# Sample states of a retention layer: keys and values of all batches in each 32-row quarter, updates by four 32-row matmuls

## The chip, the cores and the metric

The kernel runs on one core of one Trainium2 chip. The metric is the device time of one execution in microseconds (us), the median of several. TensorE is called PE in the profile, VectorE DVE, ScalarE ACT, GpSimd POOL; SP issues the DMAs.

## The reference

One layer of a decoder runs on 256 prompt tokens and on 8 sample batches of 4 new tokens each, so that 288 columns of tokens go through every product. The part that the change touches is the retention branch, for 8 heads with keys of 256 and values of 512 features. Each sample batch has a state of 256 x 512 per head, which is read, used and written back:

```python
inner = jnp.einsum('bhij,bhje->bhie', scores, v)
cross = jnp.einsum('bhid,bhde->bhie', q, S) * jnp.exp(log_g[:, None] * (i + 1.0))[None, :, :, None]
k_dec = k * jnp.exp(log_g[:, None] * (C - 1.0 - i))[None, :, :, None]
S_new = jnp.exp(log_g * C)[None, :, None, None] * S + jnp.einsum('bhjd,bhje->bhde', k_dec, v)
return S_new, inner + cross
```

For a sample batch C is 4. All else of the layer (projections, short convolution, output product, convolutional feed-forward) is dense products of 2048 or 5632 features with the 288 columns.

## The kernel before

Tokens lie on the free dimension and features on partitions. Every weight is loaded as float32, a unit of 1 MB at a time (`wunit`, L71), and split into two float32r parts, `wh` by ACT (L83) and `wl` by DVE (L84); a product then takes three matmuls of 128 rows, 128 columns and 288 streamed columns (`mm3`, L91 to L94). One unit is 48 such products. Three units of raw weights are held at a time.

The retention branch goes head by head (L516 to L541). Beside the projections of head h run the steps of `tail` of head h - 1 (L501): eight steps for the sample states, then their outputs, the gate and the product with `p_ret`. The program is given to a scheduler that fixes the order on each engine ahead of time; on the chip each engine takes its instructions strictly in that order.

For the samples of one head there are these parts:

- `krep` and the last 128 columns of `vT` hold the keys and values of the 32 sample tokens four times over. Transposed they give `ks` (L381) and `vs` (L362), 128 rows each: four quarters of 32 rows, each with all 8 batches. The quarters differ in being the high or the low part of the number, so that one matmul over 128 rows adds all four products of the parts.
- `state_cross` (L434) works on four batches at once: for each of the four and for each half `dt` of the key features, one float32 matmul of 128 rows and 32 columns, streaming 512 columns of the state, into its own 32 partitions of `pso`. The four have their own 32 columns of the array each.
- `spad` (L443) adds the scores' part to `pso` with one 128-row matmul.
- `state_update` (L445), for one batch: ACT copies `ks` to `kb` with a mask that keeps the rows of that batch (L448), PE makes two matmuls `pu` of 128 rows and 512 streamed columns (L451), DVE adds each to the decayed state (L452), and SP stores the state.
- `state_batch` (L456) loads four states ahead, runs `state_cross` at batches 0 and 4, and loads batch b + 4 when batch b is done. The state tiles `st` have five buffers (`NST`, L34), so a load for batch 5, 6 or 7 waits for an earlier store.

PSUM has three buffers with the tag `acc`, for the dense products, and five with the tag `r`, for all else: `pso` holds one of those five from the first cross product to the end of the head's samples, and the `pu` tiles use the others.

Of the kernel before, what the change touches and what calls it, by code (L numbers as in the profile page):

```python
# [34 lines left out]
J = 4  # L35
# [16 lines left out]
def tile_hybrid_step(ctx: ExitStack, tc: tile.TileContext, a, o):  # L52
# [83 lines left out]
    def rstd_tokens(sq, name):  # L136
        """1/sqrt(mean over features + eps) of each token, tokens on partitions"""
        st = psum("r", f"st_{name}")
        for c, at, _, _ in CHUNKS:
            T.matmul(st[:, c : c + 1], sq[:, at : at + P], mean, start=True, stop=True)  # L140
        tt = cp.tile([P, 3], F32, tag="stt", name=f"stt_{name}", bufs=2)
        V.tensor_scalar(out=tt, in0=st[:, 0:3], scalar1=EPS, scalar2=None, op0=ALU.add)
        r = cp.tile([P, 3], F32, tag="str", name=f"str_{name}", bufs=2)
        G.tensor_tensor(out=r, in0=tt, in1=mhalf[:, 0:3], op=ALU.pow)
        return r

    def rstd_bcast(r, name):
        """that, of all tokens on every partition (in PSUM)"""
        dg = cp.tile([P, N], F32, tag="stdg", name=f"stdg_{name}")
        rb = psum("r", f"strb_{name}")  # L150
        for c, _, n, skip in CHUNKS:
            to = slice(P * c, P * c + n)
            V.tensor_scalar(out=dg[:, to], in0=ident[:, skip:], scalar1=r[:, c : c + 1],
                            scalar2=None, op0=ALU.mult)
            T.matmul(rb[:, to], ones, dg[:, to], start=True, stop=True)  # L155
        return rb[:, :N]

# [67 lines left out]
    # ======================= retention =======================  # L225
    # The sample states of a head stream beside the projections of the next one.
# [4 lines left out]
    bmask = sp.tile([P, DEC_B], F32, name="bmask")  # L231
    nc.sync.dma_start(out=bmask, in_=a["bmask"])
    # batch g * J + j: its queries at columns 4g of block (g, j), its outputs in rows 32j + 4g
# [8 lines left out]
    def toks(t):  # L242
        return t.rearrange("p (g j t) -> p g j t", g=G2, j=J)

# [35 lines left out]
    def qk_split(hd):  # L280
        h, rot = hd.h, hd.rot
        hd.qkh = ap_.tile([P, 4, SEQ], F32R, tag="ph", name=f"qkh{h}")
        hd.qkl = ap_.tile([P, 4, SEQ], F32R, tag="pl", name=f"qkl{h}")
        S.copy(hd.qkh, rot[:, :, :SEQ])
        V.tensor_tensor(out=hd.qkl, in0=rot[:, :, :SEQ], in1=hd.qkh.bitcast(F32), op=ALU.subtract)
        hd.krep = ap_.tile([P, 2, 4, NS], F32, tag="krep", name=f"krep{h}")
        S.copy(hd.krep, rot[:, 2:4, SEQ:].unsqueeze(2).to_broadcast([P, 2, 4, NS]))

    def v_unit(hd, e):
        """v, scaled; the samples' part four times, for its exact parts."""  # L290
        if e == 0:
            hd.vT = ap_.tile([P, 4, SEQ + 4 * NS], F32, tag="vT", name=f"vT{hd.h}")
        acc = project(32 + 4 * hd.h + e, f"a_v{hd.h}_{e}")
        V.tensor_tensor(out=hd.vT[:, e, :SEQ], in0=acc[:, :SEQ], in1=rstd1[:, :SEQ], op=ALU.mult)
        V.tensor_tensor(
            out=hd.vT[:, e, SEQ:].rearrange("p (r n) -> p r n", r=4),
            in0=acc[:, SEQ:N].unsqueeze(1).to_broadcast([P, 4, NS]),
            in1=rstd1[:, SEQ:N].unsqueeze(1).to_broadcast([P, 4, NS]), op=ALU.mult,
        )

    def g_unit(hd, e):
        """silu(g) doubled, as (tanh(g/2) + 1) * g"""
        h = hd.h
        acc = project(64 + 4 * h + e, f"a_g{h}_{e}")
        gr = ap_.tile([P, N], F32, tag="gr", name=f"gr{h}_{e}")
        V.tensor_tensor(out=gr, in0=acc[:, :N], in1=rstd1, op=ALU.mult)
        th = ap_.tile([P, N], F32, tag="th", name=f"th{h}_{e}")
        S.activation(th, gr, AF.Tanh, scale=0.5)
        sge = sp.tile([P, N], F32, tag="sg", name=f"sg{h}_{e}", bufs=4)
        V.scalar_tensor_tensor(out=sge, in0=th, scalar=1.0, in1=gr, op0=ALU.add, op1=ALU.mult)  # L310
        hd.sg.append(sge)

    def scores(hd):
        """transposed, [j, i], with the decay"""
# [12 lines left out]
        for dt in range(2):  # L327
            T.matmul(scs[:, :NS], hd.krep[:, dt].rearrange("p r n -> p (r n)"), rot[:, dt, SEQ:],
                     start=dt == 0, stop=dt == 1)
# [10 lines left out]
        for q in (1, 3):  # L340
            r = slice(32 * q, 32 * q + 32)
            V.tensor_tensor(out=rows(spad)[r], in0=toks(sms)[r], in1=rows(spad)[r].bitcast(F32),
                            op=ALU.subtract)

    def q_pad(hd):
        """the samples' queries with their decay, one batch per block, zeros elsewhere"""
        h, rot = hd.h, hd.rot
        for g in range(G2):
            at = J * DEC_T * g
            V.tensor_tensor(  # L350
                out=qpad[:, :, g, :, DEC_T * g : DEC_T * g + DEC_T],
                in0=rot[:, 0:2, SEQ + at : SEQ + at + J * DEC_T].rearrange("p d (j t) -> p d j t", j=J),
                in1=qdec[:, h, at : at + J * DEC_T].rearrange("p (j t) -> p j t", j=J)
                .unsqueeze(1).to_broadcast([P, 2, J, DEC_T]), op=ALU.mult,
            )

    def v_trans(hd):
        """v with tokens on partitions"""
# [4 lines left out]
        for c in range(3):  # L363
# [7 lines left out]
            else:  # L371
                S.copy(hd.vs, tp)
                V.tensor_tensor(out=hd.vs[64:, :], in0=tp[64:, :], in1=hd.vs[64:, :].bitcast(F32),
                                op=ALU.subtract)

    def k_trans(hd):
        """k with tokens on partitions, and its decay to the end of the step"""
# [3 lines left out]
        hd.ks = sp.tile([P, DK], F32R, tag="ks", name=f"ks{h}")  # L381
        for c in range(3):
            tp = psum("r", f"tk{h}_{c}")
            for dt in range(2):
                src = hd.rot[:, 2 + dt, P * c : P * c + P] if c < 2 else hd.krep[:, dt].rearrange("p r n -> p (r n)")
# [6 lines left out]
            else:  # L392
                S.activation(hd.ks, tp[:, :DK], AF.Copy, scale=dec)
                for q in (1, 3):
                    r = slice(32 * q, 32 * q + 32)
                    V.scalar_tensor_tensor(out=hd.ks[r, :], in0=tp[r, :DK], scalar=dec[r],
                                           in1=hd.ks[r, :].bitcast(F32), op0=ALU.mult, op1=ALU.subtract)

    def prompt_out(hd):
        """outputs of the prompt, normalised per head"""  # L400
# [33 lines left out]
    def state_cross(hd, g):  # L434
        """what the states of J batches add to their outputs, side by side in the array"""
# [9 lines left out]
    def state_update(hd, b):  # L445
        h, st = hd.h, hd.st[b]
        kb = sp.tile([P, DK], F32R, tag="kb", name=f"kb{h}_{b}", bufs=2)
        S.activation(kb, hd.ks.bitcast(F32), AF.Copy, scale=bmask[:, b : b + 1])  # L448
        for dt in range(2):
            pu = psum("r", f"pu{h}_{b}{dt}")  # L450
            T.matmul(pu, kb[:, P * dt : P * dt + P], hd.vs, start=True, stop=True)  # L451
            V.scalar_tensor_tensor(out=st[:, dt, :], in0=st[:, dt, :], scalar=float(G_STEP[h]),  # L452
                                   in1=pu, op0=ALU.mult, op1=ALU.add)
        nc.sync.dma_start(out=o["ret_s"][h, b], in_=st)

    def state_batch(hd, b):  # L456
        if b == 0:
            for j in range(J):
                state_load(hd, j)
        if b % J == 0:  # L460
            state_cross(hd, b // J)
        state_update(hd, b)
        if b + J < DEC_B:
            state_load(hd, b + J)
# [9 lines left out]
    def gated(hd):  # L474
        """back to features on partitions, gated"""
# [12 lines left out]
    def p_ret_unit(hd, g):  # L488
        """this head's part of four columns of p_ret"""
# [11 lines left out]
    def tail(hd):  # L501
        """the rest of a head, in steps to go beside other products"""
        for b in range(DEC_B):
            yield lambda b=b: state_batch(hd, b)
# [39 lines left out]
    # ======================= phase B: gated short conv, merge =======================  # L544
# [92 lines left out]
    # ======================= phase C: w_o, residual =======================  # L637
# [33 lines left out]
    # the first products of the channel mixer go along with its inputs  # L671
# [61 lines left out]
    # ======================= phase D: conv FFN =======================  # L733
# [74 lines left out]
def _constants():  # L808
# [11 lines left out]
    row = np.arange(P) % NS  # L820
    for h in range(H):
# [10 lines left out]
    bmask = (b[row][:, None] == np.arange(DEC_B)[None, :]).astype(np.float32)  # L832
    return {
        "cos": np.cos(ang).astype(np.float32), "sin": np.sin(ang).astype(np.float32),
        "mask": mask, "kdec": kdec, "qdec": qdec, "bmask": bmask,
# [82 lines left out]
```

## Time and profile before

| | |
|---|---|
| three runs | 2568.78, 2570.11, 2570.53 us; median 2570.11 us |
| profiled execution, its span from first to last instruction | 2568.1 us |
| PE busy | 2536.6 us of the span |
| DVE busy | 1542.1 us |
| ACT busy | 1069.1 us |
| DMA | 474.18 MB, 185 GB/s mean |

The profile gives no time of the profiled execution but its span; the three runs stand 0.7 to 2.4 us above it. A PE record in the trace has a start and a modelled end: since matmuls follow each other in a pipeline, the time that one costs is read from the distance between its start and the start of the next, not from its duration. A float32 matmul (as in `state_cross`) has two records, a float32r matmul one.

### The profile page before, as it was taken

The numbers are of one execution on the slowest core, as the hardware profiler recorded it, in microseconds if no ns is written. First come the engines' busy times: TensorE is split into PE (matmuls) and PEld (weight loads), VectorE is DVE, ScalarE is ACT, GpSimd is POOL, SyncE is SP. The second block draws the span as 40 slices with busy tenths as digits, with TensorE's granted clock in tenths as the row PEclk, the third lists the DMA queues.
The fourth block names the chain that finished last, engine by engine and source line by source line (L and its number), as shares of the span: only waits on it lengthen the run. The fifth ranks groups of instructions, "written<-read, shape, count | busy, mean of one in ns | idle before, by whom it ended". The sixth has DMA issues, their size and how long they took to land. (4 is left out here: it accounts for less than half of the span.)

```text
span 2568.1 us, 44840 instructions
## 1 busy us (share of the span) xinstructions
PE 2536.6 (99%) x18864; PEld 2485.6 (97%) x18864; DVE 1542.1 (60%) x2349; ACT 1069.1 (42%) x1475; POOL 86.9 (3%) x244
## 2 busy tenths in 40 slices
PE   8999999999999999999999999999999999999997
PEld 8999999999999999999999999989999999999997
DVE  7565656666665656555555555477666446666644
ACT  5444444443444433333333333454444334444443
POOL 2000000000000000000000000021000000000001
PEclk9999999999999999999999999999999999999998
DMA  7565565656575746444444445434444455444453
GB/s 268 176 233 210 211 225 203 219 203 229 191 249 180 266 164 221 165 165 166 168 171 170 165 164 200 166 132 172 165 166 160 160 167 185 168 165 164 150 169 117
DMA packets 85163, 474.18 MB, mean 185 GB/s; under 512 B 10464, under 2 KB 13280, under 8 KB 43360
## 3 DMA queue, kind: packets, MB, share of 16 engines
q1 hardware_dynamic: 84960, 471.30, 52.3%
q8 instruction: 148, 2.42, 0.4%
q14 instruction: 55, 0.45, 0.1%
HBM read 430.60 MB, written 40.66 MB: 184 GB/s over the span
## 5 line engine op out<-in xcount | busy, mean ns | idle before, releaser
L83 ACT CAST wh<-raw 128x1024 fp32r<-128x1024 f32 (+2 forms) x776 | 778.7, 1004 | 1275.3 <-PE a_d L93 160.4
L84 DVE TENSOR_TENSOR wl<-raw,wh 128x1024 fp32r<-128x1024 f32 (+2 forms) x776 | 907.0, 1169 | 665.8 <-ACT wh L83 662.5
L93 PE MATMUL a_d<-fop,wh 128*128 128x288 f32 x704 | 209.1, 297 | 0.0
L92 PE MATMUL a_d<-fop,wh 128*128 128x288 f32 x704 | 208.4, 296 | 0.0
L94 PE MATMUL a_d<-fop,wl 128*128 128x288 f32 x704 | 206.3, 293 | 0.0
L92 PE MATMUL a_gate<-h2op,wh 128*128 128x288 f32 x688 | 203.2, 295 | 0.0
L94 PE MATMUL a_gate<-h2op,wl 128*128 128x288 f32 x688 | 202.1, 294 | 1.0 <-DVE wl L84 1.0
L93 PE MATMUL a_gate<-h2op,wh 128*128 128x288 f32 x688 | 202.3, 294 | 0.0
L92 PE MATMUL a_up<-h2op,wh 128*128 128x288 f32 x672 | 198.5, 295 | 0.0
L93 PE MATMUL a_up<-h2op,wh 128*128 128x288 f32 x672 | 197.6, 294 | 0.0
L94 PE MATMUL a_up<-h2op,wl 128*128 128x288 f32 x672 | 197.3, 294 | 0.0
L92 PE MATMUL a_g<-hop,wh 128*128 128x288 f32 x512 | 152.6, 298 | 0.0
L92 PE MATMUL a_p<-yop,wh 128*128 128x288 f32 x512 | 152.5, 298 | 0.0
L93 PE MATMUL a_g<-hop,wh 128*128 128x288 f32 x512 | 152.2, 297 | 0.0
L92 PE MATMUL a_v<-hop,wh 128*128 128x288 f32 x512 | 151.3, 295 | 0.0
L92 PE MATMUL a_gt<-hop,wh 128*128 128x288 f32 x512 | 151.2, 295 | 0.0
L93 PE MATMUL a_p<-yop,wh 128*128 128x288 f32 x512 | 151.0, 295 | 0.0
L94 PE MATMUL a_p<-yop,wl 128*128 128x288 f32 x512 | 150.8, 295 | 0.0
L94 PE MATMUL a_g<-hop,wl 128*128 128x288 f32 x512 | 150.7, 294 | 0.0
L93 PE MATMUL a_gt<-hop,wh 128*128 128x288 f32 x512 | 150.5, 294 | 0.0
L93 PE MATMUL a_v<-hop,wh 128*128 128x288 f32 x512 | 150.5, 294 | 0.0
L94 PE MATMUL a_v<-hop,wl 128*128 128x288 f32 x512 | 150.4, 294 | 0.0
(270 smaller groups left out, 6636.0 us busy)
## 6 DMA issues: line engine op xcount, KB each, us to landing
raw<-in_w_in SPq DMA_DIRECT2D x173, 1024.0 KB, 4.9
raw<-in_w_down SPq DMA_DIRECT2D x64, 704.0 KB, 4.1
raw<-in_w_up SPq DMA_DIRECT2D x43, 1024.0 KB, 4.8
raw<-in_w_gate SPq DMA_DIRECT2D x43, 1024.0 KB, 4.8
st<-in_state SPq DMA_DIRECT2D x64, 512.0 KB, 3.7
out_ret_s<-st SPq DMA_DIRECT2D x64, 512.0 KB, 6.3
raw<-in_p_ret SPq DMA_DIRECT2D x32, 1024.0 KB, 4.8
raw<-in_p_conv SPq DMA_DIRECT2D x16, 1024.0 KB, 4.8
```

What stands on the lines that cost most here:

```text
L83: S.copy(wh[:, to], raw[:, of])
L84: V.tensor_tensor(out=wl[:, to], in0=raw[:, of], in1=wh[:, to].bitcast(F32), op=ALU.subtract)
L92: T.matmul(out, lh, rh, start=first, stop=False)
L93: T.matmul(out, lh, rl, start=False, stop=False)
L94: T.matmul(out, ll, rh, start=False, stop=last)
```

## The change

The samples' tokens are laid out anew on the 128 rows. Before, quarter r of the array (rows 32r to 32r + 31) held copy r of all 32 tokens. Now quarter j holds, in four blocks of 8 rows, the four copies of the tokens of batches j and 4 + j, 4 rows each. So the four copies of one batch, with the high and low parts, lie in one quarter. The constants on the host follow (`kdec`, the samples' part of `mask`), and `rmask` takes the place of `bmask`: two columns that choose high or low part, two that choose the batches 0 to 3 or 4 to 7.

- `krep` is filled by four ACT copies in place of one, and the samples' part of `vT` by two DVE products per tile in place of one.
- the low parts of `spad`, `vs` and the keys are made with `rmask` on all rows.
- `kb` is made once for each group of four batches in `k_trans` (two tiles per head, beside the tile `kd`), not once per batch. `ks` is gone.
- an update is a matmul of 32 rows, 128 columns and 512 streamed columns. The number of update matmuls stays 16 per head, 128 in all.
- `state_step` replaces `state_batch`: step 0 loads the states of batches 0 to 3 and makes the first cross products, step 2 updates all four batches, stores them and loads batches 4 to 7, step 4 makes the second cross products, step 6 the second updates and stores.

```diff
-        hd.krep = ap_.tile([P, 2, 4, NS], F32, tag="krep", name=f"krep{h}")
-        S.copy(hd.krep, rot[:, 2:4, SEQ:].unsqueeze(2).to_broadcast([P, 2, 4, NS]))
+        hd.krep = ap_.tile([P, 2, J, 4, G2, DEC_T], F32, tag="krep", name=f"krep{h}")
+        for dt in range(2):
+            for g in range(G2):
+                S.copy(hd.krep[:, dt, :, :, g, :], batches(rot[:, 2 + dt, SEQ:], g))
...
-                S.activation(hd.ks, tp[:, :DK], AF.Copy, scale=dec)
-                for q in (1, 3):
-                    r = slice(32 * q, 32 * q + 32)
-                    V.scalar_tensor_tensor(out=hd.ks[r, :], in0=tp[r, :DK], scalar=dec[r],
-                                           in1=hd.ks[r, :].bitcast(F32), op0=ALU.mult, op1=ALU.subtract)
+                kd = ap_.tile([P, DK], F32, tag="kd", name=f"kd{h}")
+                S.activation(kd, tp[:, :DK], AF.Copy, scale=dec)
+                S.copy(hd.kb[0], kd)
+                V.scalar_tensor_tensor(out=kd, in0=hd.kb[0].bitcast(F32), scalar=rmask[:, 0:1], in1=kd,
+                                       op0=ALU.mult, op1=ALU.add)
+                for g in range(G2):
+                    S.activation(hd.kb[g], kd, AF.Copy, scale=rmask[:, 2 + g : 3 + g])
...
-    def state_update(hd, b):
-        h, st = hd.h, hd.st[b]
-        kb = sp.tile([P, DK], F32R, tag="kb", name=f"kb{h}_{b}", bufs=2)
-        S.activation(kb, hd.ks.bitcast(F32), AF.Copy, scale=bmask[:, b : b + 1])
+    def state_update(hd, g):
+
+        h = hd.h
         for dt in range(2):
-            pu = psum("r", f"pu{h}_{b}{dt}")
-            T.matmul(pu, kb[:, P * dt : P * dt + P], hd.vs, start=True, stop=True)
-            V.scalar_tensor_tensor(out=st[:, dt, :], in0=st[:, dt, :], scalar=float(G_STEP[h]),
-                                   in1=pu, op0=ALU.mult, op1=ALU.add)
-        nc.sync.dma_start(out=o["ret_s"][h, b], in_=st)
...
+            pus = []
+            for j in range(J):
+                pu = psum("r", f"pu{h}_{g}{dt}{j}")
+                r = slice(32 * j, 32 * j + 32)
+                T.matmul(pu, hd.kb[g][r, P * dt : P * dt + P], hd.vs[r, :], start=True, stop=True)
+                pus.append(pu)
+            for j, pu in enumerate(pus):
+                st = hd.st[J * g + j]
+                V.scalar_tensor_tensor(out=st[:, dt, :], in0=st[:, dt, :], scalar=float(G_STEP[h]),
+                                       in1=pu, op0=ALU.mult, op1=ALU.add)
+
+    def state_step(hd, i):
+
+        if i == 0:
             for j in range(J):
                 state_load(hd, j)
-        if b % J == 0:
-            state_cross(hd, b // J)
-        state_update(hd, b)
-        if b + J < DEC_B:
-            state_load(hd, b + J)
+        if i in (0, 4):
+            state_cross(hd, i // 4)
+        if i in (2, 6):
+            state_update(hd, i // 4)
+            for j in range(J):
+                nc.sync.dma_start(out=o["ret_s"][hd.h, J * (i // 4) + j], in_=hd.st[J * (i // 4) + j])
+        if i == 2:
+            for j in range(J):
+                state_load(hd, J + j)
```

The scheduler places the new steps in another way among the dense products. The first place is the second half of a head's samples on PE (head 2, beside the projections `a_v` of head 3). Before, the eight cross products `pso` of batches 4 to 7 follow each other, and the two updates `pu` of batch 4 stand right behind them:

```order
L94 MATMUL a_v_0_4058<-hop_93,wl_1_4055 128x288
L440 MATMUL pso_3794<-st_4_3813,qpad 32x512
L440 MATMUL pso_3794<-st_5_3890,qpad 32x512
L440 MATMUL pso_3794<-st_6_3962,qpad 32x512
L440 MATMUL pso_3794<-st_7_4039,qpad 32x512
L440 MATMUL pso_3794<-st_4_3813,qpad 32x512
L440 MATMUL pso_3794<-st_5_3890,qpad 32x512
L440 MATMUL pso_3794<-st_6_3962,qpad 32x512
L440 MATMUL pso_3794<-st_7_4039,qpad 32x512
L451 MATMUL pu_40_4119<-vs_3266,kb_4_4117 128x512
L451 MATMUL pu_41_4122<-vs_3266,kb_4_4117 128x512
```

Now two of the eight stand before ten dense products:

```order
L94 MATMUL a_v_0_4054<-hop_93,wl_1_4051 128x288
L450 MATMUL pso_3795<-st_4_3960,qpad 32x512
L450 MATMUL pso_3795<-st_5_3962,qpad 32x512
L92 MATMUL a_v_1_4124<-hop_78,wh_0_4116 128x288
L93 MATMUL a_v_1_4124<-hop_78,wh_0_4116 128x288
```

Behind those ten stands one cross product alone:

```order
L94 MATMUL a_v_1_4124<-hop_80,wl_0_4117 128x288
L92 MATMUL a_v_1_4124<-hop_81,wh_0_4116 128x288
L450 MATMUL pso_3795<-st_6_3964,qpad 32x512
L93 MATMUL a_v_1_4124<-hop_81,wh_0_4116 128x288
L94 MATMUL a_v_1_4124<-hop_81,wl_0_4117 128x288
```

And 29 dense products later come the other five:

```order
L94 MATMUL a_v_1_4124<-hop_90,wl_1_4121 128x288
L450 MATMUL pso_3795<-st_7_3966,qpad 32x512
L450 MATMUL pso_3795<-st_4_3960,qpad 32x512
L450 MATMUL pso_3795<-st_5_3962,qpad 32x512
L450 MATMUL pso_3795<-st_6_3964,qpad 32x512
L450 MATMUL pso_3795<-st_7_3966,qpad 32x512
L92 MATMUL a_v_1_4124<-hop_91,wh_1_4120 128x288
```

So the cross products of the second group of batches, one block before, are three now.

The second place is the updates of that group on PE. Before they go two or four at a time between units of dense products; here are those of batches 5 and 6:

```order
L451 MATMUL pu_50_4189<-vs_3266,kb_5_4187 128x512
L451 MATMUL pu_51_4192<-vs_3266,kb_5_4187 128x512
L451 MATMUL pu_60_4198<-vs_3266,kb_6_4196 128x512
L451 MATMUL pu_61_4201<-vs_3266,kb_6_4196 128x512
```

Now the four matmuls of the first half of the keys (`pu_100` to `pu_103`: group 1, half 0, quarters 0 to 3) stand side by side, and those of the second half (`pu_110` to `pu_113`), from 24 dense products later, one by one:

```order
L463 MATMUL pu_110_4188<-vs_3267,kb_1_3180 128x512
L92 MATMUL a_v_2_4214<-hop_86,wh_1_4210 128x288
L463 MATMUL pu_111_4190<-vs_3267,kb_1_3180 128x512
L93 MATMUL a_v_2_4214<-hop_86,wh_1_4210 128x288
L94 MATMUL a_v_2_4214<-hop_86,wl_1_4211 128x288
L463 MATMUL pu_112_4192<-vs_3267,kb_1_3180 128x512
L92 MATMUL a_v_2_4214<-hop_87,wh_1_4210 128x288
```

Of the 128 updates, 15 times four stand next to each other, once five, 7 times two, and 49 stand alone. Before, they stood in 50 pairs and 7 fours.

The third place is the DMA queue of SP at the stores and loads of the same kind of states. Before, each load of a state is followed by weights (`raw`) before the next store:

```order
L454 DMA out_ret_s<-st_0_3786 128x1024
L431 DMA st_5_3890<-in_state 128x1024
L75 DMA raw_4048<-in_w_in 128x2048
L75 DMA raw_4126<-in_w_in 128x2048
L454 DMA out_ret_s<-st_1_3788 128x1024
L431 DMA st_6_3962<-in_state 128x1024
L75 DMA raw_4205<-in_w_in 128x2048
```

Now three stores go out one behind the other, and four loads follow with a single unit of weights among them:

```order
L480 DMA out_ret_s<-st_0_3787 128x1024
L480 DMA out_ret_s<-st_1_3789 128x1024
L480 DMA out_ret_s<-st_2_3791 128x1024
L441 DMA st_5_3962<-in_state 128x1024
L480 DMA out_ret_s<-st_3_3793 128x1024
L441 DMA st_6_3964<-in_state 128x1024
L75 DMA raw_4266<-in_w_in 128x2048
L441 DMA st_7_3966<-in_state 128x1024
L441 DMA st_0_5079<-in_state 128x1024
```

The states' transfers, which were spread over the units of a head, stand in a bunch now, and each load still stands behind the store whose buffer it takes.

More of the change, by code (lines that the diff above doesn't have):

```diff
@@ L230, in tile_hybrid_step @@
     ap_ = astack.enter_context(tc.tile_pool(name="ap", bufs=1))
-    bmask = sp.tile([P, DEC_B], F32, name="bmask")
-    nc.sync.dma_start(out=bmask, in_=a["bmask"])
+    rmask = sp.tile([P, 4], F32, name="rmask")
+    nc.sync.dma_start(out=rmask, in_=a["rmask"])
     qpad = sp.tile([P, 2, G2, J, 32], F32, name="qpad")
@@ L243, in toks, with batches @@
         return t.rearrange("p (g j t) -> p g j t", g=G2, j=J)
+    def batches(t, g):
+        u = t.rearrange("p (g j t) -> p g j t", g=G2, j=J)[:, g]
+        return u.unsqueeze(2).to_broadcast([P, J, 4, DEC_T])
     sel = sp.tile([P, NS], F32, name="sel")
@@ L294, in v_unit @@
         V.tensor_tensor(out=hd.vT[:, e, :SEQ], in0=acc[:, :SEQ], in1=rstd1[:, :SEQ], op=ALU.mult)
[L295 to L299, printed above, removed]
+        for g in range(G2):
+            V.tensor_tensor(
+                out=hd.vT[:, e, SEQ:].rearrange("p (j r g t) -> p j r g t", j=J, r=4, g=G2)[:, :, :, g, :],
+                in0=batches(acc[:, SEQ:N], g), in1=batches(rstd1[:, SEQ:N], g), op=ALU.mult,
+            )
     def g_unit(hd, e):
@@ L327, in scores @@
         for dt in range(2):
-            T.matmul(scs[:, :NS], hd.krep[:, dt].rearrange("p r n -> p (r n)"), rot[:, dt, SEQ:],
+            T.matmul(scs[:, :NS], hd.krep[:, dt].rearrange("p j r g t -> p (j r g t)"), rot[:, dt, SEQ:],
                      start=dt == 0, stop=dt == 1)
@@ L339, in scores @@
         S.copy(rows(spad), toks(sms))
-        for q in (1, 3):
-            r = slice(32 * q, 32 * q + 32)
-            V.tensor_tensor(out=rows(spad)[r], in0=toks(sms)[r], in1=rows(spad)[r].bitcast(F32),
-                            op=ALU.subtract)
+        for g in range(G2):
+            V.scalar_tensor_tensor(out=rows(spad)[:, g], in0=rows(spad)[:, g].bitcast(F32), scalar=rmask[:, 0:1],
+                                   in1=toks(sms)[:, g], op0=ALU.mult, op1=ALU.add)
     def q_pad(hd):
@@ L372, in v_trans @@
                 S.copy(hd.vs, tp)
-                V.tensor_tensor(out=hd.vs[64:, :], in0=tp[64:, :], in1=hd.vs[64:, :].bitcast(F32),
-                                op=ALU.subtract)
+                V.scalar_tensor_tensor(out=hd.vs, in0=hd.vs.bitcast(F32), scalar=rmask[:, 1:2], in1=tp,
+                                       op0=ALU.mult, op1=ALU.add)
     def k_trans(hd):
@@ L380, in k_trans @@
         hd.kl = ap_.tile([P, 2, DK], F32R, tag="kl", name=f"kl{h}")
-        hd.ks = sp.tile([P, DK], F32R, tag="ks", name=f"ks{h}")
+        hd.kb = [sp.tile([P, DK], F32R, tag="kb", name=f"kb{h}_{g}", bufs=G2) for g in range(G2)]
         for c in range(3):
@@ L384, in k_trans @@
             for dt in range(2):
-                src = hd.rot[:, 2 + dt, P * c : P * c + P] if c < 2 else hd.krep[:, dt].rearrange("p r n -> p (r n)")
+                src = hd.rot[:, 2 + dt, P * c : P * c + P] if c < 2 else hd.krep[:, dt].rearrange("p j r g t -> p (j r g t)")
                 T.transpose(tp[:, P * dt : P * dt + P], src, ident)
@@ L392, in k_trans @@
             else:
-                S.activation(hd.ks, tp[:, :DK], AF.Copy, scale=dec)
-                for q in (1, 3):
-                    r = slice(32 * q, 32 * q + 32)
-                    V.scalar_tensor_tensor(out=hd.ks[r, :], in0=tp[r, :DK], scalar=dec[r],
-                                           in1=hd.ks[r, :].bitcast(F32), op0=ALU.mult, op1=ALU.subtract)
+                kd = ap_.tile([P, DK], F32, tag="kd", name=f"kd{h}")
+                S.activation(kd, tp[:, :DK], AF.Copy, scale=dec)
+                S.copy(hd.kb[0], kd)
+                V.scalar_tensor_tensor(out=kd, in0=hd.kb[0].bitcast(F32), scalar=rmask[:, 0:1], in1=kd,
+                                       op0=ALU.mult, op1=ALU.add)
+                for g in range(G2):
+                    S.activation(hd.kb[g], kd, AF.Copy, scale=rmask[:, 2 + g : 3 + g])
     def prompt_out(hd):
@@ L443, in state_cross @@
             T.matmul(hd.pso, spad, hd.vs, start=False, stop=False)
-    def state_update(hd, b):
-        h, st = hd.h, hd.st[b]
-        kb = sp.tile([P, DK], F32R, tag="kb", name=f"kb{h}_{b}", bufs=2)
-        S.activation(kb, hd.ks.bitcast(F32), AF.Copy, scale=bmask[:, b : b + 1])
+    def state_update(hd, g):
+        h = hd.h
         for dt in range(2):
-            pu = psum("r", f"pu{h}_{b}{dt}")
-            T.matmul(pu, kb[:, P * dt : P * dt + P], hd.vs, start=True, stop=True)
-            V.scalar_tensor_tensor(out=st[:, dt, :], in0=st[:, dt, :], scalar=float(G_STEP[h]),
-                                   in1=pu, op0=ALU.mult, op1=ALU.add)
-        nc.sync.dma_start(out=o["ret_s"][h, b], in_=st)
-    def state_batch(hd, b):
-        if b == 0:
+            pus = []
[10 more added lines that the diff above has]
+        if i == 0:
             for j in range(J):
                 state_load(hd, j)
-        if b % J == 0:
-            state_cross(hd, b // J)
-        state_update(hd, b)
-        if b + J < DEC_B:
-            state_load(hd, b + J)
+        if i in (0, 4):
[7 more added lines that the diff above has]
+                state_load(hd, J + j)
     def sample_out(hd):
@@ L501, in tail @@
     def tail(hd):
-        for b in range(DEC_B):
-            yield lambda b=b: state_batch(hd, b)
+        for i in range(DEC_B):
+            yield lambda i=i: state_step(hd, i)
         yield lambda: sample_out(hd)
@@ L819, in _constants @@
     b = np.arange(NS) // DEC_T
-    row = np.arange(P) % NS
+    at = np.arange(P)
+    row = DEC_T * (J * (at // DEC_T % G2) + at // 32) + at % DEC_T
     for h in range(H):
@@ L831, in _constants @@
         qdec[:, h, :] = _exp32(LOG_G[h] * (t + 1).astype(np.float32))[None, :]
-    bmask = (b[row][:, None] == np.arange(DEC_B)[None, :]).astype(np.float32)
+    part = np.arange(P) // 8 % 4
+    group = np.arange(P) // DEC_T % G2
+    rmask = np.stack([-(part % 2), -(part // 2), group == 0, group == 1], axis=1).astype(np.float32)
     return {
         "cos": np.cos(ang).astype(np.float32), "sin": np.sin(ang).astype(np.float32),
-        "mask": mask, "kdec": kdec, "qdec": qdec, "bmask": bmask,
+        "mask": mask, "kdec": kdec, "qdec": qdec, "rmask": rmask,
     }
```

## The prediction

> **What bounds the kernel now.** I read the page first: its busy times, and then the chain that ended last.
>
> ```profile
> PE 2536.6 (99%) x18864; PEld 2485.6 (97%) x18864; DVE 1542.1 (60%) x2349; ACT 1069.1 (42%) x1475; POOL 86.9 (3%) x244
> PE 32%; DVE 1%; ACT 0%; POOL 0%; issue 0%; DVEq 0%; POOLq 0%
> ```
>
> PE is busy for 99% of the span, and the chain is made of PE alone but for a hundredth. Busy time says little by itself, since matmul durations overlap, so the second view is the busy time of the stretch with the samples' work, here 100 to 1010 us.
>
> ```profile
> 100.00:1010.00 910.00, 909.65 (x6656) 863.34 (x6655) 558.89 (x859) 382.04 (x554) 11.30 (x26) 1.00 0.61 215
> ```
>
> The columns after the length are PE, weight loads, DVE, ACT and POOL, then clock, DMA share and GB/s. PE has no hole: 909.65 of 910 us, at the full clock; DVE and ACT have over 350 us of air each. The third view is the timeline of PE, where the distance from start to start is what a matmul costs. Here is one block of eight cross products, and behind it a pair of updates.
>
> ```profile
> 377.77 0.30 PE L92 MATMUL a_v<-hop,wh 128*128 128x288 f32 x1
> 377.90 0.29 PE L93 MATMUL a_v<-hop,wh 128*128 128x288 f32 x1
> 378.03 0.29 PE L94 MATMUL a_v<-hop,wl 128*128 128x288 f32 x1
> 378.26 1.92 PE L440 MATMUL pso<-st,qpad 128*32 128x512 f32 x16
> 380.11 0.73 PE L451 MATMUL pu<-vs,kb 128*128 128x512 f32 x2
> 380.69 0.30 PE L92 MATMUL a_v<-hop,wh 128*128 128x288 f32 x1
> ```
>
> A dense product costs 0.13 us, the eight cross products (16 records) 1.85 us. So whatever the change adds to PE's own work in this stretch, or takes from it, moves the end by as much; work on other engines counts only where PE comes to wait for it.
>
> **The updates, before.** Four updates in the dense stream:
>
> ```profile
> 386.90 0.29 PE L94 MATMUL a_v<-hop,wl 128*128 128x288 f32 x1
> 387.03 1.09 PE L451 MATMUL pu<-vs,kb 128*128 128x512 f32 x4
> 387.96 0.29 PE L92 MATMUL a_v<-hop,wh 128*128 128x288 f32 x1
> ```
>
> 387.96 - 387.03 = 0.93 us, 0.2325 us each, and nothing extra ahead (0.13 us) or behind. 128 updates cost 128 x 0.2325 = 29.8 us. That is all the change can win, and four side by side in the best case leave a quarter of it.
>
> **The price of a switch of the array's shape.** No row of before has a matmul of 32 rows. The nearest are the cross products, which use 32 columns each with several side by side. First a block of six cross products, then one of two:
>
> ```profile
> 332.90 0.29 PE L93 MATMUL a_p<-yop,wh 128*128 128x288 f32 x1
> 333.04 0.29 PE L94 MATMUL a_p<-yop,wl 128*128 128x288 f32 x1
> 333.26 1.91 PE L440 MATMUL pso<-st,qpad 128*32 128x512 f32 x12
> 335.10 0.40 PE L92 MATMUL a_p<-yop,wh 128*128 128x288 f32 x1
> 335.34 0.30 PE L93 MATMUL a_p<-yop,wh 128*128 128x288 f32 x1
> 335.48 0.29 PE L94 MATMUL a_p<-yop,wl 128*128 128x288 f32 x1
> ...
> 341.42 0.29 PE L94 MATMUL a_p<-yop,wl 128*128 128x288 f32 x1
> 341.64 1.05 PE L440 MATMUL pso<-st,qpad 128*32 128x512 f32 x4
> 342.63 0.50 PE L443 MATMUL pso<-vs,spad 128*128 128x512 f32 x1
> ```
>
> The first block works on the column groups 0, 1, 2, 3, 0, 1 and lasts 335.10 - 333.26 = 1.84 us, the second on 2, 3 and lasts 342.63 - 341.64 = 0.99 us. The eight above took 1.85 us. So a set of up to four side by side costs 1.84 - 0.99 = 0.85 us whether two or four groups work in it: a block is paid by sets, not by matmuls. And there is a fixed price per block: 0.99 - 0.85 = 0.14 at its end, 0.09 at its start (341.64 - 341.42 = 0.22 in place of 0.13), and 0.10 on the first dense product behind it (335.34 - 335.10 = 0.24 in place of 0.14). Together **0.33 us for going into the other shape and back**.
>
> **The cross products, after.** The first block of a head keeps its pieces. The second, one block of two sets in before, is cut up in the program's order. Heads 1 to 7 have 2, 1 and 5 cross products: 1 + 1 + 2 = 4 sets (the five name batch 7 twice) and three switches. Against two sets and one switch that is 2 x 0.85 + 2 x 0.33 = 2.36 us, for seven heads 16.52 us. Head 0 has 1, 1, 1 and 5: five sets and four switches, 3 x 0.85 + 3 x 0.33 = 3.54 us more. Sum **+20.1 us**. A block of a single column has no row of its own; its two records run in the same column, so I take a whole set, and as the low end half of one (0.43 us less for each of ten such blocks, 4.3 us in all).
>
> **The updates, after.** A matmul of 32 rows still streams 512 columns, so alone it costs 0.23 us as before, and only neighbours share. By the program's order heads 1 to 6 have nine separate groups each (2, 4, 1, 1, 4 and four single ones), head 0 has ten, head 7 eight: 72 groups, of which only the one of five needs a second turn. Streaming is 72 x 0.23 + 0.23 = 16.8 us. Whether a group pays the switch isn't in the trace. Low end: nothing, and the updates cost 16.8 - 29.8 = -13.0 us. Value taken: the 0.33 us of the column blocks, which is the nearest row and the same act, a part of the array used between products of the whole: 72 x 0.33 = 23.8 us, so 16.8 + 23.8 - 29.8 = **+10.8 us**. High end: the four weight loads of a group go one after the other too. Four short matmuls that each load all 128 columns:
>
> ```profile
> 65.43 0.58 PE L328 MATMUL scs<-rot,krep 128*128 128x32 f32 x4
> 65.84 0.38 PE L92 MATMUL a_g<-hop,wh 128*128 128x288 f32 x1
> ```
>
> 0.41 us for four, so 0.10 us a load. Three more loads in 15 fours, four in the five, one in seven pairs: 56 x 0.10 = 5.6 us more.
>
> The Trainium skill, "TensorEngine Tiling (Array Packing)", Key Properties, says that going from one tiling mode to another drains the array, and that other tiles of the same mode do not. It speaks against this change, whose groups mostly stand alone between whole-array products; the 0.33 us of the column blocks agrees, and no run so far shows row quarters. By that rule the updates pay as in the value taken.
>
> The Trainium skill, "TensorE: Matmul & The Clock Gate", Part 3, gives 3.07 times for four 32-row tiles with 512 columns. As an estimate from that page a group of four would cost 0.93 / 3.07 = 0.30 us, not 0.23, one microsecond more over 15 fours.
>
> **The other engines.**
>
> ```profile
> L448 ACT ACTIVATE kb<-ks,bmask 128x256 fp32r<-128x256 f32 x64 | 31.7, 506 | 17.5 <-PE pu L451 17.5
> L452 DVE SCALAR_TENSOR_TENSOR st<-st,pu 128x512 f32<-128x512 f32 x128 | 81.4, 682 | 32.1 <-PE pu L451 32.1
> L84 DVE TENSOR_TENSOR wl<-raw,wh 128x1024 fp32r<-128x1024 f32 (+2 forms) x776 | 907.0, 1169 | 665.8 <-ACT wh L83 662.5
> L295 DVE TENSOR_TENSOR vT<-a_v,rstd 128x128 f32<-128x128 f32 x32 | 9.0, 280 | 0.0
> ```
>
> ACT loses most of the 64 masked copies (31.7 us), and gets small ones; DVE makes 32 more short products of `vT`, at most 9.0 us. Neither is on PE's path now, and the air of the stretch covers both. I put them at nothing. If that cover went (a split of weights late by a copy's 0.5 us, once per head), it would be 4 us. The evictions cost 0.68 us each, and PSUM leaves four buffers beside `pso`: four are filled by one group, so a fifth update waits for the first eviction. The order puts 21 to 24 dense products, 2.7 to 3.1 us, between, and the first eviction needs about 0.4 + 0.7 us and at worst a split ahead of it (1.2 us); this fits.
>
> **Sum.** +20.1 + 10.8 = **+30.9 us** on the profiled span of 2568.1 us. The runs stand 0.7 to 2.4 us above that span, the median 2.0; the addition is the same for them: 2570.1 + 30.9 = **2601 us**, 1.2% more.
>
> **Rivals.**
>
> *Row quarters switch for free.* They write into whole PSUM rows as the full array does, which speaks for it; the column blocks speak against it. Then -13.0 + 20.1 = +7.1 us, 2577 us. If single columns also cost half a set, +2.8 us, 2573 us.
>
> *States come late.* SP now sends the stores in a bunch, and the loads stand behind them.
>
> ```profile
> st<-in_state SPq DMA_DIRECT2D x64, 512.0 KB, 3.7
> out_ret_s<-st SPq DMA_DIRECT2D x64, 512.0 KB, 6.3
> SPq L431 <- DMA out_ret_s<-st: 251.2, 59, 8.2
> ```
>
> Count from the group of four updates in the middle (`pu` 002, 003, 010, 011). Batch 0 is evicted third, at 0.4 + 3 x 0.68 = 2.4 us; store 6.3, load 3.7: batch 5 is there at 12.4 us. PE needs it after 96 dense products and two single updates, 96 x 0.13 + 2 x 0.56 = 13.6 us. The margin is 1.2 us. Already SP waits 4.3 us for each store (251.2 over 59). One more transfer of 512 KB ahead, at the stretch's 215 GB/s 2.4 us, would cost 1.2 us a head, 10 us; two would cost 3.6 us a head, 29 us. PE, being in order, takes the dense products behind with it. With the serial loads 2607 us, with this 2611 to 2630 us.
>
> *Faster: lone updates vanish beside their neighbours.* A single update occupies a quarter of the rows; if it ran while the dense products before and behind it fill and empty the array, a group would cost less than its 0.23 us of streaming. It pays back the cross products at (29.8 - 20.1) / 72 = 0.135 us a group, and makes the kernel faster by over 0.2% below 0.06 us. At nothing it gives 2570.1 - 9.7 = 2560 us. Dense products leave no room for it in the trace: they follow each other at 0.13 us with PE and weight loads at 95% and more.
>
> *It doesn't do what it says.* In part this is no rival but a term: 49 of 128 updates stand alone.
>
> **How the numbers follow.** Forecast 2601 us, chance 0.53 (its own range 2592 to 2607); late states or serial loads 0.19; free switches 0.20; free switches with cheap single columns 0.04; faster 0.04. What a measurement can tell from no change is about 0.2%, 5.1 us. The free switches at +7.1 us lie just above that, so I give half of them to "same": same 0.10 + 0.04 = 0.14, faster 0.04, slower 0.82. The range takes in the free switches below, and above a part of the late states: 2576 to 2616 us.
>
> **What would show it.** In the changed kernel's timeline, a single `pu` (L463) between dense products: from the start of the product ahead of it to that of the second product behind it 0.13 + 0.23 + 0.13 = 0.49 us if the switch is free, 0.82 us if it is paid. Four of them: starts a few ns apart and about 0.23 us in all, or 0.10 us apart. The second cross blocks of a head: 0.99, 0.99 and 1.84 us. Waits of `pso` for `st`: 2 us in all or fewer, or many in heads 0 to 7 if the states are late. The forecast is wrong if PE's waits in this stretch grow beyond a few us, or if the groups stand differently from the order.

## The result, and the profile after

The changed kernel takes 2607.0 us (median of four runs, 2605.96 to 2608.58), the one before 2569.48 us (the three runs above and one more): 1.0146 times as long, interval 1.0133 to 1.0158. That is 37.5 us slower.

First the page and the stretch of the samples' work, as read before: the busy times, then PE, weight loads, DVE, ACT and POOL from 100 to 1046 us.

```profile
PE 2572.7 (99%) x18864; PEld 2481.1 (95%) x18864; DVE 1540.7 (59%) x2373; ACT 1052.4 (40%) x1459; POOL 85.6 (3%) x244
```

```profile
100.00:1046.00 946.00, 946.00 (x6658) 859.94 (x6658) 558.79 (x882) 364.86 (x534) 11.16 (x26) 1.00 0.57 207
```

PE is as full as before, with the same number of instructions on it, and the mean clock of the stretch is 1.00 as before. DVE and ACT are a little less busy. So PE didn't come to wait for another engine: its own work takes longer. The timeline of PE says where. A group of four updates, a single update, and a block of one cross product (two records), each with the dense products around it:

```profile
372.61 0.29 PE L94 MATMUL a_qk<-hop,wl 128*128 128x288 f32 x1
372.83 0.50 PE L463 MATMUL pu<-vs,kb 32*128 32x512 f32 x4
373.27 0.40 PE L92 MATMUL a_qk<-hop,wh 128*128 128x288 f32 x1
373.51 0.30 PE L93 MATMUL a_qk<-hop,wh 128*128 128x288 f32 x1
...
376.01 0.29 PE L94 MATMUL a_qk<-hop,wl 128*128 128x288 f32 x1
376.24 0.49 PE L463 MATMUL pu<-vs,kb 32*128 32x512 f32 x1
376.66 0.40 PE L92 MATMUL a_qk<-hop,wh 128*128 128x288 f32 x1
376.90 0.29 PE L93 MATMUL a_qk<-hop,wh 128*128 128x288 f32 x1
...
389.70 0.29 PE L92 MATMUL a_v<-hop,wh 128*128 128x288 f32 x1
389.93 1.04 PE L450 MATMUL pso<-st,qpad 128*32 128x512 f32 x2
390.90 0.40 PE L93 MATMUL a_v<-hop,wh 128*128 128x288 f32 x1
391.14 0.29 PE L94 MATMUL a_v<-hop,wl 128*128 128x288 f32 x1
```

Read the starts. The single update stands 376.66 - 376.24 = 0.42 us before the next product, the four together 0.44 us: the quarters do run side by side, and four cost nearly what one costs. But 0.23 us pass ahead of the group (0.13 between dense products) and 0.24 us behind the first product after it. From the product ahead to the second one behind, the single update takes 376.90 - 376.01 = 0.89 us, where 0.13 + 0.23 + 0.13 = 0.49 us would do without a switch. A group pays about **0.39 us** for its shape (0.385 by the nanoseconds of the starts). The single cross product costs 390.90 - 389.93 = 0.97 us, as much as a whole set with its end, and has 0.1 us ahead and 0.1 us behind like the others. The two other blocks of the same head, of two and of five cross products, are these:

```profile
387.42 1.05 PE L450 MATMUL pso<-st,qpad 128*32 128x512 f32 x4
388.40 0.40 PE L92 MATMUL a_v<-hop,wh 128*128 128x288 f32 x1
...
394.94 1.90 PE L450 MATMUL pso<-st,qpad 128*32 128x512 f32 x10
396.77 0.40 PE L92 MATMUL a_v<-hop,wh 128*128 128x288 f32 x1
```

They cost 0.98 and 1.83 us. So three blocks take 0.98 + 0.97 + 1.83 us, and one block took 1.85 us before.

The states' loads took twice as long to land as before (3.7 us), the stores less (6.3 us before):

```profile
st<-in_state SPq DMA_DIRECT2D x64, 512.0 KB, 7.5
out_ret_s<-st SPq DMA_DIRECT2D x64, 512.0 KB, 3.6
```

Yet no cross product waited for a state: by the landings in the trace, each state of batches 5 to 7 was there 2.3 us or more before the first cross product that reads it. Here is what the weight loads of `pso` (L450) sat idle for, with no DMA among it:

```profile
L450 PEldq EVENT_SEMAPHORE  x8: 51/51/51, 102.1 to 968.8; - x8
its engine sat idle before it (us, times) until:
  issue: 16.1, 70
  PE a_qk L93: 0.2, 1
  PE a_p L93: 0.2, 1
```

The kernel before did have such a wait, which the busy time of its stretch hides. In the first of its heads a block of eight took 137.51 - 134.26 = 3.25 us in place of 1.85, because the state of batch 7 came late:

```profile
134.26 1.06 PE L440 MATMUL pso<-st,qpad 128*32 128x512 f32 x6
135.68 1.90 PE L440 MATMUL pso<-st,qpad 128*32 128x512 f32 x10 [0.35 <-DMA st<-in_state]
137.51 0.73 PE L451 MATMUL pu<-vs,kb 128*128 128x512 f32 x2
```

### The profile page after: what moved, and what is told of

The parts are those of the page before. It is cut to its first block, busy times and chain, and to the rows that moved or that the text cites. A ratio compares the mean times of both kernels' runs of the same rounds, so it can differ in the third digit from the quotient of the medians.

```text
span 2604.2 us, 44852 instructions
## 1 busy us (share of the span) xinstructions
PE 2572.7 (99%) x18864; PEld 2481.1 (95%) x18864; DVE 1540.7 (59%) x2373; ACT 1052.4 (40%) x1459; POOL 85.6 (3%) x244
## 5 line engine op out<-in xcount | busy, mean ns | idle before, releaser
L92 PE MATMUL a_v<-hop,wh 128*128 128x288 f32 x512 | 155.5, 304 | 0.0
L93 PE MATMUL a_v<-hop,wh 128*128 128x288 f32 x512 | 153.7, 300 | 0.0
```

Of the source, the lines that this page charges most:

```text
L92: T.matmul(out, lh, rh, start=first, stop=False)
L93: T.matmul(out, lh, rl, start=False, stop=False)
```

## The experiments

The kernel before was run again with them: 2569.25 us, the median of ten runs, with the first four experiments, and 2569.14 us, of twelve, with the last.

Three theories stood after this reading. A: the price lies in going from the whole array to row quarters or column groups and back, once per group. B: single updates are dear because they wait for PSUM buffers that DVE must empty. C: all of the loss is the cutting up of the cross products.

### The same order, updates over all rows

One line of the changed kernel is edited, so that order, waits and cross products stay. The updates of a batch then add all four batches of its group, so the states written are not the reference's.

```diff
-                r = slice(32 * j, 32 * j + 32)
+                r = slice(0, P)
```

> The changed kernel, with each update matmul over all 128 rows in place of the 32 of its quarter (the masked keys then add the four batches of a group, so the states written are not the reference's). PE's order, all waits and the cut-up cross products stay. Theory A (each group of row-quarter updates pays about 0.09 us before it, 0.19 at its end and 0.10 behind it): the switches of 72 groups go, the updates cost 128 x 0.2325 = 29.8 us in place of 44.9, so 2607 - 15 = 2592 us, and what is left over the kernel before, about 22 us, is the cross products' cut. Rival B (the single updates are dear because they wait for free PSUM buffers): 2607 us, or more, since fours now take 0.93 us. Rival C (all of the loss is the cross products' cut): 2607 us or a little more.

Measured: 2590.35 us, 1.0082 of the kernel before (1.0067 to 1.0098), 16.6 us less than the changed kernel. PE's order is row for row that of the changed kernel. A single update in its timeline:

```profile
372.17 0.30 PE L94 MATMUL a_qk<-hop,wl 128*128 128x288 f32 x1
372.30 0.39 PE L463 MATMUL pu<-vs,kb 128*128 128x512 f32 x1
372.54 0.29 PE L92 MATMUL a_qk<-hop,wh 128*128 128x288 f32 x1
372.67 0.30 PE L93 MATMUL a_qk<-hop,wh 128*128 128x288 f32 x1
```

372.67 - 372.17 = 0.50 us, against 0.89 us for the same update on a quarter. It waits for the same buffers and pays nothing, so B falls. The waits agree: in the changed kernel the weight loads of `pu` sat idle for an eviction (DVE `st`) twice, 1.0 us in all.

```profile
  DVE st L467: 1.0, 2
```

The 21.1 us that remain over the kernel before come with the order, in which the cross products are cut up; by the starts of the blocks in the changed kernel's trace, that cut costs 19.8 us. C explains these and no more.

### The new layout in the old order

Here the steps of the kernel before are back, batch by batch, with the updates on the batch's quarter. PE's order is that of before almost row for row (the cross products whole, 50 pairs and 7 fours of updates); the two updates of a pair lie in the same quarter and can't share.

```diff
-    def state_update(hd, g):
+    def state_update(hd, b):
...
+        r = slice(32 * (b % J), 32 * (b % J) + 32)
         for dt in range(2):
...
+            T.matmul(pu, hd.kb[b // J][r, P * dt : P * dt + P], hd.vs[r, :], start=True, stop=True)
```

> The new layout, with the steps of the kernel before: batch by batch, two 32-row updates per batch, both in the same quarter, and the cross products whole. Theory A: 57 groups x 0.37 us of switch = 21 us, less 8 x 0.2 us where a group stands right behind a cross block, and nothing shared inside a group: 2569.5 + 20 = 2589 us. Rival B (waits of single updates) and rival C (only the cross products' cut costs): 2569 to 2571 us. If two loads of weights into the same quarter can't overlap, 64 x 0.1 us on top of A: 2596 us.

Measured: 2587.04 us, 1.0070 (1.0056 to 1.0083), 17.8 us slower than before with the cross products untouched. So the shape alone costs time, and C as the whole cause falls. A pair:

```profile
377.31 0.29 PE L94 MATMUL a_qk<-hop,wl 128*128 128x288 f32 x1
377.53 0.73 PE L461 MATMUL pu<-vs,kb 32*128 32x512 f32 x2
378.19 0.40 PE L92 MATMUL a_v<-hop,wh 128*128 128x288 f32 x1
378.43 0.30 PE L93 MATMUL a_v<-hop,wh 128*128 128x288 f32 x1
```

378.43 - 377.31 = 1.12 us for 0.13 + 2 x 0.23 + 0.13 = 0.72 us of work: 0.40 us, the price of one group and not of two. So it is paid per change of shape. The second update of the pair adds 0.66 - 0.42 = 0.24 us, its streaming alone, so the second weight load into the same quarter costs nothing of its own, and the 2596 us of the expectation are out. The 2 us below the expectation have a simple source, mostly: the seven fours hold batches 5 and 6 in two quarters, which share, and that wasn't counted. By the starts they take 0.67 us, not 4 x 0.23 + 0.19 = 1.11 us; 3 us less, of which the price of 0.39 in place of 0.37 us per group takes back 1.

### The two halves in two steps

`state_update` is called for one half of the keys at a time, in steps 2 and 3, and 6 and 7.

```diff
-        if i in (2, 6):
-            state_update(hd, i // 4)
+        if k in (2, 3):
+            state_update(hd, g, (2, 3).index(k))
```

> The changed kernel, with the two halves of a group's updates in two steps (2 and 3, 6 and 7), so that the second four are not sent singly. PE's order then has 46 groups of updates, not 72, and the second cross products of a head in four blocks (1, 1, 1, 5), not three. Theory A: updates 46 x 0.62 = 28.5 us in place of 44.9, cross blocks 7 x 1.2 us more: 2607 - 16 + 8 = 2599 us. Rival B: the single updates are gone, and so is the loss but for the cross blocks: 2590 us. Rival C: 2607 + 8 = 2615 us.

Measured: 2597.36 us, 1.0109 (1.0095 to 1.0123), 9.6 us less than the changed kernel, where A said 8. Fewer groups (46) save, and more cross blocks (four per head) give back about 8 us of the 16 by A's count. B (2590 us) and C (2615 us) are out here too.

### The updates right behind the cross products

The same halves, in steps 0 and 1, and 4 and 5, with the stores and loads behind them. The stores and loads then go out a step earlier, and the scheduler leaves the second cross products of a head in one block. 39 groups of updates, 25 of them fours.

```diff
-        if i in (2, 6):
-            state_update(hd, i // 4)
+        if k in (0, 1):
+            state_update(hd, g, (0, 1).index(k))
...
-        if i == 2:
+        if i == 1:
             for j in range(J):
                 state_load(hd, J + j)
```

> The changed kernel, with the updates of the first half of the keys in the step of the cross products (0 and 4) and those of the second half in the next (1 and 5), the stores and loads behind them. PE's order then has 39 groups of updates, 25 of them fours, and the second cross products whole as in the kernel before. Theory A: updates 39 x 0.62 = 24.2 us, less 8 x 0.2 us shared with a cross block ahead, in place of 29.8 before: 2569.5 - 7 = 2563 us, 0.25% faster than the kernel before. Rival (the states now arrive in a bunch and PE waits for them): 2566 to 2580 us, with waits of pso for st in the trace.

Measured: 2561.49 us, 0.9970 (0.9959 to 0.9982): **faster than both**, by 45.5 us than the changed kernel and by 7.8 us than the one before, where A said 2563 us. About 1.4 us of the 7.8 are the wait for a state in the trace of the kernel before, which this order's trace doesn't have; whether all runs have it isn't known. A cross block with a group of four behind it:

```profile
495.25 0.29 PE L94 MATMUL a_v<-hop,wl 128*128 128x288 f32 x1
495.48 1.92 PE L450 MATMUL pso<-st,qpad 128*32 128x512 f32 x16
497.33 0.51 PE L462 MATMUL pu<-vs,kb 32*128 32x512 f32 x4
497.77 0.40 PE L92 MATMUL a_v<-hop,wh 128*128 128x288 f32 x1
498.00 0.30 PE L93 MATMUL a_v<-hop,wh 128*128 128x288 f32 x1
```

The block of eight costs 497.33 - 495.48 = 1.85 us as before, the four behind it 0.44 us, and the price ahead and behind (0.23 and 0.23 us in place of 0.13) is paid once for both. Four whole-array updates cost 0.93 us before. The loads of the states land later still:

```profile
st<-in_state SPq DMA_DIRECT2D x64, 512.0 KB, 8.1
```

No cross product waits for one (all eight blocks of the second group last 1.85 us), so the rival of late states falls in this order too.

### The scores' matmul out of the way

The whole-array matmul with `spad` stood between the first cross products of a head and its first updates. Here it goes ahead of both, on top of the edit above.

```diff
         if g == 0:
-            T.matmul(hd.pso, spad, hd.vs, start=False, stop=False)
+            T.matmul(hd.pso, spad, hd.vs, start=True, stop=False)
```

> The kernel of e6_early, with the whole-array matmul of the scores (spad) ahead of the first cross products of a head, not between them and the first updates. Theory A (the price is paid where the shape of the array changes, and a block of columns next to a group of row quarters shares it): per head one change from columns to the whole array and one from the whole array to rows go, 0.2 us where the spad matmul lay and 0.2 us at the join: 8 x 0.4 = 3 us, so 2558.5 us. Rival (the price is one per block, whatever stands beside it): 2561.5 us as e6_early.

> The kernel of e6_early once more, on the same chip as e7_spad: 2561.5 us.

Measured: 2560.19 us (0.9966 of the kernel before, 0.9954 to 0.9979), against 2561.67 us for the kernel without this edit on the same chip. By the runs it is half of what A expected. In the traces the stretch from the first dense product behind the start's three units to the last update shows the difference without the start; the rows, the kernel without the edit first, have durations and then the first and last start:

```profile
L92 PE MATMUL a_s<-hop,wh x16: 293/296/298, 31.0 to 37.6; 128*128 128x288 f32 x16
L462 PE MATMUL pu<-vs,kb x128: 488/497/500, 107.0 to 986.5; 32*128 32x512 f32 x128
```

```profile
L92 PE MATMUL a_s<-hop,wh x16: 293/296/298, 31.9 to 38.5; 128*128 128x288 f32 x16
L462 PE MATMUL pu<-vs,kb x128: 489/497/500, 107.7 to 985.3; 32*128 32x512 f32 x128
```

986.5 - 31.0 = 955.5 us became 985.3 - 31.9 = 953.4 us, 2.1 us less, while this execution's start had taken 0.9 us longer. So the join saves, by 2.1 us where 3 were expected. The end of the column block is still paid there: with a pair of updates right behind it, a block of three cross products, one set, takes 339.09 - 338.10 = 0.99 us, as blocks of one set took ahead of the whole array.

```profile
338.10 1.06 PE L452 MATMUL pso<-st,qpad 128*32 128x512 f32 x6
339.09 0.50 PE L462 MATMUL pu<-vs,kb 32*128 32x512 f32 x2
```

The intervals of the two kernels against the one before overlap; that the second is the faster one rests on the trace more than on the runs.

## Why the prediction was right, and where its sizes were off

The forecast was 2601 us, the result 2607.0 us; +30.9 us were expected and 37.5 measured. The result lies at the upper end of the forecast's own range (2592 to 2607 us). 2607 us is also the number that the prediction gives for serial weight loads, and that is chance: the loads are not serial.

**PE is the bound, and its own work decides.** Right. No wait of another engine or of a transfer shows that could make up the loss (of the idle time of the weight loads of `pu`, 2.4 us in all are put down to DVE); the stretch grew because PE's instructions cost more. That PE had no hole before was not quite so: the wait of 1.4 us for a state stood in it.

**The order.** Right as read from the program: 72 groups of updates, the second cross products in three or four blocks. Nothing on the chip moves them.

**The cross products, +20.1 us.** Right. The kernel with whole-array updates in the same order is 21.1 us over the kernel before. The three blocks of a head were forecast at 0.99, 0.99 and 1.84 us and take 0.98, 0.97 and 1.83 us. A block with a single column costs a whole set, as was taken; the low end, half a set, is out.

**The updates, +10.8 us.** The mechanism was right, the term too small. The price of a change of shape was taken from the column blocks, 0.33 us; for row quarters it is 0.39 us. 72 x (0.23 + 0.39) + 0.23 - 29.8 = +15.1 us. The experiment that takes away the quarters alone gives 16.6 us by the runs. The 4.3 us of this term are most of the 6.6 us that were missing. The high end, weight loads one after the other, is out: four loads go at once.

**The sum with the measured price** is 20.1 + 15.1 = 35.2 us. At the last product of the stretch (`a_p`, started at 1072.7 us before and at 1108.1 us after) the traces differ by 35.4 us. In this lie two things that the sum doesn't have, and they nearly cancel. The wait of 1.4 us of the kernel before is gone. And for 3.4 us of the changed kernel's profiled execution the granted clock fell to half, with PE busy without a gap. Here is a window of 4 us around it, with PE busy, clock, DMA share and GB/s, and two products from it:

```profile
782.00:786.00 4.00, 4.00 (x19) 0.57 1.06 305
```

```profile
782.27 0.45 PE L94 MATMUL a_v<-hop,wl 128*128 128x288 f32 x1
782.51 0.45 PE L92 MATMUL a_v<-hop,wh 128*128 128x288 f32 x1
```

Fourteen dense products stand 0.24 us apart there in place of 0.13, which is 1.5 us. No other run's trace has such a place before 1680 us, and why it is there isn't known. So part of the 16.6 us above may be the clock and not the quarters.

The whole span grew by 36.1 us (2568.1 to 2604.2), so 0.7 us lie behind this stretch. Between the spans and the runs lie 1.4 us more, and these are a matter of which execution was profiled. Most runs stand about 1.8 us above their own span. The profiled execution of the changed kernel is its fastest run, 1.0 us under the median, and the span of 2568.1 us before would belong to a run of 2569.9 us, 0.4 us over its median.

**Free switches** (2577 us): out, by the 0.89 us of the single update. **Faster** (a lone update costs nothing beside its neighbours): out, by the same row. **Late states**: the transfer part came true, the loads land in 7.5 us where 3.7 had been assumed, but PE did not wait. The stores, which had been taken at 6.3 us, land in 3.6 us, and so by the medians the sum of a store and a load is 11.1 us where 10.0 us had been reckoned; the margin of 1.2 us held. This was luck in part: that the stores would get shorter wasn't foreseen, and with 6.3 us for them the same count would have made the state 2.6 us late. The count had taken a load's time of before for one that has others around it.

**The rule.** The Trainium skill, "TensorEngine Tiling (Array Packing)", Key Properties, says that changing the tiling mode drains the array. The runs agree in so far as each change has a price, and add its size, 0.39 us a group; the draining itself no trace here shows. The other figure of the Trainium skill, of "TensorE: Matmul & The Clock Gate", Part 3, 3.07 times for four tiles, gave 0.30 us as an estimate for a group of four. The group stands 0.44 us before the next product, and with its margins 0.93 us of whole-array updates become 0.44 + 0.09 + 0.10 = 0.63 us, 1.5 times. So the gain of the figure is not reached by one group between whole-array products.

## What to carry to other kernels

In a dense stream like this one, matmuls on a part of the array save only if several stand side by side: each group of them costs a fixed price, 0.39 us, more than a whole-array update (0.23 us). Four side by side gain, one alone loses. So count the groups in the order that the scheduler made, not the matmuls in the code. And an edit that moves steps can cut up neighbours it doesn't touch: more than half of this loss lay in cross products whose code is the same; steps placed so that four updates go out at once and right behind the cross products turned a loss of 37.5 us into a gain of 8 to 9 us.

## What the runs showed of the hardware

Four row quarters are started 3 to 4 ns apart in the trace, and the group stands 0.44 us before the next product where one quarter alone stands 0.42 us: four weight loads of 32 rows and 128 columns (0.18 us each) run at once. The end of a group costs more than that of a column block: 0.42 - 0.23 = 0.19 us against 0.97 - 0.85 = 0.12 us. Why was not tried. Two different part shapes that follow each other, columns and then quarters, without the whole array between, share the 0.1 us ahead and the 0.1 us behind; the column block's end is paid all the same (0.99 us for one set, 1.85 us for two, with quarters behind as with the whole array). The granted clock can fall to half in the midst of a full stream on PE: it did once, for 3.4 us, in one of eight traces.
